# A streamed relu-and-sum: partition pitches of 60 KB and 452 KB in place of 512 KB, and early sums stored by SyncE

## The chip, the cores and the metric

The kernel runs on one core of a Trainium2 chip. The metric is device time in microseconds (us) of one execution. Most executions of one kernel agree within 0.3%.

A ratio below is the mean time of one kernel's fast runs over the mean time of the other's fast runs of the same rounds, so it is not quite the ratio of the medians that stand beside it. An interval is the 95% interval of that ratio.

## The reference

```python
def setup_inputs():
    batch, seq, dim = 32, 512, 1024
    return {"x": np.random.randn(batch, seq, dim).astype(np.float32)}

def reference(x):
    relu_x = np.maximum(x, 0)
    return np.sum(relu_x, axis=-1).astype(np.float32)
```

These are 16,384 rows of 4 KB, 67.11 MB of input, and one float per row of output. Each of the 128 partitions gets 128 rows.

## The kernel before

Each partition owns 128 consecutive rows, so its data in HBM starts 128 x 4 KB = 512 KB after that of the partition before it. That distance is the pitch. SyncE issues all loads: seven chunks of 16 rows a partition in two buffers, then 8, 4, 2 and 1 rows, then the last row in four pieces. ACT and DVE reduce alternate rows.

```python
xv = x_flat.rearrange("(p m) d -> p (m d)", p=P)              # pitch 512 KB
out2d = out.rearrange("b s -> (b s)").rearrange("(p m) -> p m", p=P)
big, tail, pieces = 16, [8, 4, 2, 1], [244, 252, 260, 268]    # (three lines, shortened)
# ... cut: pools, act_op and dve_op (relu with a running sum into one column of res)
for j, cpd in enumerate(chunks):
    # ... cut: xt = a tile of cpd rows; 8 rows and more from the two "io" buffers
    nc.sync.dma_start(out=xt, in_=xv[:, m0 * D : (m0 + cpd) * D].rearrange("p (c d) -> p c d", c=cpd))
    for c in range(cpd):
        m = m0 + c
        if m == NT - 2:
            act_op(xt[:, c, :], xt[:, c, :], m)
            nc.scalar.dma_start(out=out2d[:, 0 : NT - 2], in_=res[:, 0 : NT - 2])
        elif (c % 2) == 0:
            act_op(xt[:, c, :], xt[:, c, :], m)
        else:
            dve_op(xt[:, c, :], xt[:, c, :], res[:, m : m + 1])
    m0 += cpd
# ... cut: four pieces of the last row, loaded by SyncE and summed by DVE
nc.sync.dma_start(out=out2d[:, NT - 2 : NT], in_=res[:, NT - 2 : NT])
```

The scheduler puts ACT's store ahead of its last row, since the store needs only the first 126 columns.

## Time and profile before

| | before |
|---|---|
| median of the first 3 runs | 163.6 us (163.25 to 163.61) |
| span in the profile | 161.5 us |
| input at 433.7 GB/s (pace of the median 64 KB packet) | 154.7 us |
| first load packet starts, last one ends | 1.02 us, 158.12 us |
| DVE's last operations | 157.58 to 159.18 us |

The first view is the profile's page of the kernel before: the busy time of the two computing engines, the DMA rows in 40 equal slices (tenths of busy time, then GB/s), the DMA queues (packets, MB, share of the 16 engines' time), and the chain of waits that ended last.

```profile
span 161.5 us, 347 instructions
DVE 74.3 (46%) x134; ACT 69.0 (43%) x129; POOL 0.2 (0%) x4
...
DMA  8997997996997997997996997997997997999990
GB/s 308 471 503 308 487 487 308 503 503 292 503 503 308 487 503 325 471 519 308 471 519 296 487 503 325 471 503 341 454 503 341 454 503 308 430 438 406 406 359 22
...
q1 hardware_dynamic: 2304, 67.11, 96.9%
q10 hardware_dynamic: 144, 0.06, 0.1%
q14 instruction: 2, 0.02, 0.0%
...
DMA 79%; DVE 18%; SPq 1%; issue 0%; DVEq 0%
DMA xt<-in_x_dram 62%; DVE xt L79 17%; DMA p<-in_x_dram 17%; SPq L95 1%; DVE p L79 1%; DVEq L79 0%; DVEq L16 0%
```

The DMA engines are busy 96.9% of the span with the loads, and neither computing engine reaches half. The swing between 300 and 500 in the GB/s row is no real swing: a 64 KB packet lasts 2.4 us and a slice 4.0 us, so a packet counts wholly in one slice. The rate has to be read from packets: the trace's record of each packet gives 896 packets of 64 KB with a median of 2.418 us, and 16 x 65,536 bytes / 2.418 us is 433.7 GB/s. The 17% of "DVE xt" in the chain are releases of a buffer; they do not delay the stream, because the other buffer's load is still running.

The second view is the timeline at the end of the kernel before (start in us, duration in us, engine and operation; in brackets the idle time before it and what ended it).

```profile
157.27 0.37 ACTq L103 DMA_DIRECT2D out_dram<-res  x1
157.58 0.41 DVE L79 TENSOR_SCALAR_CACHE_REDUCE p<-p 128x244 f32<-128x244 f32 x1 [0.40 <-DMA p<-in_x_dram]
...
158.64 0.19 ACT L71 ACTIVATION_READ_ACCUMULATOR xt<-xt 128x1 f32 x1
158.74 0.43 DVE L79 TENSOR_SCALAR_CACHE_REDUCE p<-p 128x271 f32<-128x271 f32 x1
...
159.25 0.35 SPq L128 DMA_DIRECT2D out_dram<-res  x1
```

DVE starts the first piece when it lands, works without a break to 159.18 us, and the last store follows. ACT ends at 158.83 us, 0.35 us ahead of DVE, although it spends 0.37 us on issuing its store.

### The profile page before, as it was taken

What the parts mean: (1) busy time and instruction counts of PE and PEld (TensorE: products, weight loads), DVE (VectorE), ACT (ScalarE), POOL (GpSimd) and SP (SyncE); (2) the same over time, 40 slices, a digit from 0 to 9 for tenths busy, and PEclk for the clock granted to TensorE, in tenths of its full rate; (3) what the DMA queues carried; (4) which work ended last, traced back from release to release, by engine and by line L of the source; (5) the groups of instructions that cost most, each with busy time, mean ns of one, the idle gap of its engine ahead of it and who ended that gap; (6) DMA issues with size and microseconds to landing.
All of it is one profiled execution on the core that took longest, in us unless ns stands there. A gap on an engine that the chain in (4) does not pass through costs nothing.

```text
span 161.5 us, 347 instructions
## 1 busy us (share of the span) xinstructions
DVE 74.3 (46%) x134; ACT 69.0 (43%) x129; POOL 0.2 (0%) x4
## 2 busy tenths in 40 slices
DVE  0000049700695008940099101991039900598983
ACT  3000049500693008920099001990039700596882
POOL 0000000000000000000000000000000000000000
DMA  8997997996997997997996997997997997999990
GB/s 308 471 503 308 487 487 308 503 503 292 503 503 308 487 503 325 471 519 308 471 519 296 487 503 325 471 503 341 454 503 341 454 503 308 430 438 406 406 359 22
DMA packets 2450, 67.19 MB, mean 416 GB/s; under 512 B 528, under 2 KB 1040, under 8 KB 1168
## 3 DMA queue, kind: packets, MB, share of 16 engines
q1 hardware_dynamic: 2304, 67.11, 96.9%
q10 hardware_dynamic: 144, 0.06, 0.1%
q14 instruction: 2, 0.02, 0.0%
HBM read 67.11 MB, written 0.07 MB: 416 GB/s over the span
## 4 chain that ended last, share of the span: by engine, by line
DMA 79%; DVE 18%; SPq 1%; issue 0%; DVEq 0%
DMA xt<-in_x_dram 62%; DVE xt L79 17%; DMA p<-in_x_dram 17%; SPq L95 1%; DVE p L79 1%; DVEq L79 0%; DVEq L16 0%
## 5 line engine op out<-in xcount | busy, mean ns | idle before, releaser
L79 DVE TENSOR_SCALAR_CACHE_REDUCE xt<-xt 128x1024 f32<-128x1024 f32 x63 | 72.6, 1216 | 84.5 <-DMA xt<-in_x_dram 84.2
L71 ACT ACTIVATE xt<-xt 128x1024 f32<-128x1024 f32 x64 | 66.7, 1043 | 89.0 <-DMA xt<-in_x_dram 89.0
L71 ACT ACTIVATION_READ_ACCUMULATOR xt<-xt 128x1 f32 x64 | 11.9, 187 | 0.0
L79 DVE DVE_READ_ACCUMULATOR xt<-xt 128x1 f32 x63 | 5.2, 83 | 0.0
L79 DVE TENSOR_SCALAR_CACHE_REDUCE p<-p 128x244 f32<-128x244 f32 (+3 forms) x4 | 1.6, 420 | 0.4 <-DMA p<-in_x_dram 0.4
L71 ACT ACT_TABLE_LOAD x1 | 1.3, 1283 | 0.8 <-PEq L143 0.8
L79 DVE DVE_READ_ACCUMULATOR p<-p 128x1 f32 x4 | 0.3, 82 | 0.0
L143 POOL MEMSET const-bfloat16-1.0<- 128x1 bf16 x1 | 0.1, 101 | 0.0
L143 POOL MEMSET const-uint8-127<- 128x1 uint8 x1 | 0.1, 101 | 0.0
L143 POOL MEMSET const-float32-0.0<- 128x1 f32 x1 | 0.1, 98 | 0.2 <-issue 0.2
L143 POOL MEMSET const-float32-1.0<- 128x1 f32 x1 | 0.1, 98 | 0.0
## 6 DMA issues: line engine op xcount, KB each, us to landing
xt<-in_x_dram SPq DMA_DIRECT2D x1, 4096.0 KB, 19.6
xt<-in_x_dram SPq DMA_DIRECT2D x1, 2048.0 KB, 24.2
xt<-in_x_dram SPq DMA_DIRECT2D x1, 1024.0 KB, 26.2
xt<-in_x_dram SPq DMA_DIRECT2D x1, 512.0 KB, 27.0
p<-in_x_dram SPq DMA_DIRECT2D x1, 134.0 KB, 10.0
p<-in_x_dram SPq DMA_DIRECT2D x1, 130.0 KB, 26.5
p<-in_x_dram SPq DMA_DIRECT2D x1, 126.0 KB, 26.7
p<-in_x_dram SPq DMA_DIRECT2D x1, 122.0 KB, 26.8
```

Of the source, the lines that this page charges most:

```text
L71: nc.scalar.activation(out=out_ap, in_=in_ap, func=mybir.ActivationFunctionType.Relu, accum_out=res[:, m : m + 1],)
L79: nc.vector.tensor_scalar(out=out_ap, in0=in_ap, scalar1=0.0, scalar2=None, op0=mybir.AluOpType.max, op1=mybir.AluOpType.add, accum_out=ac ...
L95: nc.sync.dma_start(out=xt, in_=xv[:, m0 * D : (m0 + cpd) * D].rearrange("p (c d) -> p c d", c=cpd),)
L143: nc = _bacc.Bacc("TRN2", target_bir_lowering=False, num_devices=1)
```

## The change

The intent is to take the pitch off a large power of two. The input is cut into a first block, where each partition has 15 rows (pitch 15 x 4 KB = 60 KB), and the rest, where it has 113 (pitch 452 KB). The first load has 15 rows; six of 16 and loads of 9, 4, 2 and 1 rows follow. The sums exist in two tiles, and SyncE stores the early ones in two transfers after the last load. The core of the diff, shortened:

```diff
-    xv = x_flat.rearrange("(p m) d -> p (m d)", p=P)
-    out2d = out.rearrange("b s -> (b s)").rearrange("(p m) -> p m", p=P)
-    tail = [8, 4, 2, 1]
+FIRST = 15
+TAIL = [9, 4, 2, 1]
+    cut = P * FIRST
+    xa = x_flat[:cut].rearrange("(p m) d -> p m d", p=P)
+    xb = x_flat[cut:].rearrange("(p m) d -> p m d", p=P)
+    # outa and outb likewise
@@ loads
+    nc.sync.dma_start(out=xt[:, :FIRST, :], in_=xa)
+    for n in [BIG] * nbig + TAIL:
+        nc.sync.dma_start(out=xt[:, :n, :], in_=xb[:, m0 : m0 + n, :])
@@ stores
-                nc.scalar.dma_start(out=out2d[:, 0 : NT - 2], in_=res[:, 0 : NT - 2])
+    nc.sync.dma_start(out=outa, in_=resa)
+    nc.sync.dma_start(out=outb[:, : M - 2], in_=resb[:, : M - 2])
 # (cut: tiles, the pieces and the last store, which stay as they were)
```

The 9-row load has a tile of its own; the 8-row load took one of the two large buffers.

More of the change, by code (lines that the diff above doesn't have):

```diff
@@ L10 @@
 EARLY = 1
+FIRST = 15
+BIG = 16
+TAIL = [9, 4, 2, 1]
+PIECES = [244, 252, 260, 268]
 def kernel(tc: tile.TileContext, x: bass.AP, out: bass.AP):
@@ L17, with trace_relu_sum, act, dve @@
     issue_ahead_of_the_barrier(tc, EARLY)
+@with_exitstack
+def trace_relu_sum(
+    ctx: ExitStack,
+    tc: tile.TileContext,
+    x: bass.AP,
+    out: bass.AP,
+):
+    nc = tc.nc
+    fp32 = mybir.dt.float32
+    P = nc.NUM_PARTITIONS
+    x_flat = x.flatten_outer_dims()
+    N, D = x_flat.shape
+    NT = N // P
+    assert N == P * NT and sum(PIECES) == D
+    nbig, rem = divmod(NT - FIRST - sum(TAIL) - 1, BIG)
+    assert rem == 0
+    cut = P * FIRST
+    xa = x_flat[:cut].rearrange("(p m) d -> p m d", p=P)
+    xb = x_flat[cut:].rearrange("(p m) d -> p m d", p=P)
+    out1d = out.rearrange("b s -> (b s)")
+    outa = out1d[:cut].rearrange("(p m) -> p m", p=P)
+    outb = out1d[cut:].rearrange("(p m) -> p m", p=P)
+    io = ctx.enter_context(tc.tile_pool(name="io", bufs=2))
+    small = ctx.enter_context(tc.tile_pool(name="small", bufs=1))
+    resa = small.tile([P, FIRST], fp32)
+    resb = small.tile([P, NT - FIRST], fp32)
+    def act(ap, accum_out):
+        nc.scalar.activation(
+            out=ap,
+            in_=ap,
+            func=mybir.ActivationFunctionType.Relu,
+            accum_out=accum_out,
+        )
+    def dve(ap, accum_out):
+        nc.vector.tensor_scalar(
+            out=ap,
+            in0=ap,
+            scalar1=0.0,
+            scalar2=None,
+            op0=mybir.AluOpType.max,
+            op1=mybir.AluOpType.add,
+            accum_out=accum_out,
+        )
+    def rows(xt, n, res, m0):
+        for c in range(n):
+            (act if c % 2 == 0 else dve)(xt[:, c, :], res[:, m0 + c : m0 + c + 1])
+    xt = io.tile([P, BIG, D], fp32, tag="io", name="first")
+    nc.sync.dma_start(out=xt[:, :FIRST, :], in_=xa)
+    rows(xt, FIRST, resa, 0)
+    m0 = 0
+    for n in [BIG] * nbig + TAIL:
+        if n == BIG:
+            xt = io.tile([P, BIG, D], fp32, tag="io", name=f"big{m0}")
+        else:
+            xt = small.tile([P, n, D], fp32, name=f"t{n}")
+        nc.sync.dma_start(out=xt[:, :n, :], in_=xb[:, m0 : m0 + n, :])
+        rows(xt, n, resb, m0)
+        m0 += n
+    M = NT - FIRST
+    assert m0 == M - 1
+    np_ = len(PIECES)
+    parts = []
+    col = 0
+    for i, w in enumerate(PIECES):
+        extra = np_ - 1 if i == np_ - 1 else 0
+        pt = small.tile([P, w + extra], fp32, name=f"p{i}")
+        nc.sync.dma_start(out=pt[:, :w], in_=xb[:, M - 1, col : col + w])
+        parts.append(pt)
+        col += w
+    nc.sync.dma_start(out=outa, in_=resa)
+    nc.sync.dma_start(out=outb[:, : M - 2], in_=resb[:, : M - 2])
+    last, w = parts[-1], PIECES[-1]
+    for i in range(np_ - 1):
+        dve(parts[i], last[:, w + i : w + i + 1])
+    dve(last, resb[:, M - 1 : M])
+    nc.sync.dma_start(out=outb[:, M - 2 :], in_=resb[:, M - 2 :])
@@ L36, in issue_ahead_of_the_barrier @@
     opening[at:at] = loads
-@with_exitstack
-def trace_relu_sum(
-    ctx: ExitStack,
-    tc: tile.TileContext,
-    x: bass.AP,
-    out: bass.AP,
-):
-    nc = tc.nc
-    fp32 = mybir.dt.float32
-    P = nc.NUM_PARTITIONS
-    x_flat = x.flatten_outer_dims()
-    N, D = x_flat.shape
-    assert N % P == 0
-    NT = N // P
-    xv = x_flat.rearrange("(p m) d -> p (m d)", p=P)
-    out2d = out.rearrange("b s -> (b s)").rearrange("(p m) -> p m", p=P)
-    big = 16
-    tail = [8, 4, 2, 1]
-    pieces = [244, 252, 260, 268]
-    assert sum(pieces) == D
-    nbig, rem = divmod(NT - sum(tail) - 1, big)
-    assert rem == 0
-    chunks = [big] * nbig + tail
-    io_pool = ctx.enter_context(tc.tile_pool(name="io", bufs=2))
-    res_pool = ctx.enter_context(tc.tile_pool(name="res", bufs=1))
-    res = res_pool.tile([P, NT], fp32)
-    def act_op(in_ap, out_ap, m):
-        nc.scalar.activation(
-            out=out_ap,
-            in_=in_ap,
-            func=mybir.ActivationFunctionType.Relu,
-            accum_out=res[:, m : m + 1],
-        )
-    def dve_op(in_ap, out_ap, accum_out):
-        nc.vector.tensor_scalar(
-            out=out_ap,
-            in0=in_ap,
-            scalar1=0.0,
-            scalar2=None,
-            op0=mybir.AluOpType.max,
-            op1=mybir.AluOpType.add,
-            accum_out=accum_out,
-        )
-    m0 = 0
-    for j, cpd in enumerate(chunks):
-        if cpd >= 8:
-            xt = io_pool.tile([P, cpd, D], fp32, tag="io", name=f"xt{j}")
-        else:
-            xt = io_pool.tile([P, cpd, D], fp32, tag=f"t{cpd}", bufs=1, name=f"xt{j}")
-        nc.sync.dma_start(
-            out=xt,
-            in_=xv[:, m0 * D : (m0 + cpd) * D].rearrange("p (c d) -> p c d", c=cpd),
-        )
-        for c in range(cpd):
-            m = m0 + c
-            if m == NT - 2:
-                act_op(xt[:, c, :], xt[:, c, :], m)
-                nc.scalar.dma_start(out=out2d[:, 0 : NT - 2], in_=res[:, 0 : NT - 2])
-            elif (c % 2) == 0:
-                act_op(xt[:, c, :], xt[:, c, :], m)
-            else:
-                dve_op(xt[:, c, :], xt[:, c, :], res[:, m : m + 1])
-        m0 += cpd
-    m_last = m0
-    assert m_last == NT - 1
-    base = m_last * D
-    np_ = len(pieces)
-    wlast = pieces[-1] + (np_ - 1)
-    ptiles = []
-    col = 0
-    for i, w in enumerate(pieces):
-        shape_w = w if i < np_ - 1 else wlast
-        pt = io_pool.tile([P, shape_w], fp32, tag=f"p{i}", bufs=1, name=f"p{i}")
-        ptiles.append(pt)
-        nc.sync.dma_start(out=pt[:, 0:w], in_=xv[:, base + col : base + col + w])
-        col += w
-    last = ptiles[-1]
-    for i in range(np_ - 1):
-        dve_op(ptiles[i], ptiles[i], last[:, pieces[-1] + i : pieces[-1] + i + 1])
-    dve_op(last, last, res[:, m_last : m_last + 1])
-    nc.sync.dma_start(out=out2d[:, NT - 2 : NT], in_=res[:, NT - 2 : NT])
```

## The prediction

> **What bounds it now.** The input stream. The profile's DMA row is at 9 tenths or more in nearly all 40 slices; the chain of waits is 79% DMA and 18% DVE; DVE is busy 46%, ACT 43%. In the packet records of the trace 896 packets of 64 KB carry the big loads, median 2.418 us each; 16 engines at that pace are 433.7 GB/s. So 67.11 MB need 154.7 us; the first packet starts at 1.02 us and the last piece's packets end at 158.12 us. Only about 2.4 us of the stream is not at full pace. Then come the DVE's piece sums (chain: 157.58 to 159.18 us), the last store, and the end at 161.5 us.
>
> **The intent, costed.** The pitch between partitions is now 512 KB. The Trainium skill, page "DMA: Bandwidth & Descriptors", section "Latency and other measured facts", lists 207 GB/s per direction at a 512 KiB pitch against 214 with a padded one, about 3%. This trace does not show that loss: the same page ("Where 436 GB/s comes from") gives a ceiling of 435 GB/s, and the median packet runs at 433.7. What could be pitch is the packets over 2.5 us, 26 of 896: the first on each engine takes about 3.0 us (2.55 to 3.24), 0.6 us too long; seven more, near 11.3 to 12.1 us, average 0.2 us too long. I think the first packet pays a start-up latency, not the pitch: the following packets keep the spacing and the offsets between engines, yet take 2.42 us. Were it all pitch, the stream would gain 0.6 to 0.9 us.
>
> **What moves.** The first load has 15 rows (60 KB a partition), then six of 16, then 9, 4, 2, 1 and the pieces; from the 9-row chunk on the landings come where they came before (148.6, 153.5, 155.95 us). A 16-row chunk takes 9.2 us to reduce and 19.4 us to load, so buffers come free in time. The 9-row chunk no longer waits for a buffer; that gains nothing, since the queue is never empty. ACT gets five of its rows instead of four and starts the 4-row chunk 0.5 us late, but no longer issues the 63 KB store (0.37 us at 157.27 us): it ended at 158.8 us, now about 158.4. DVE ended at 159.18 us, so ACT is off the path.
>
> SyncE issues two early stores, near 148.7 us (7.5 KB) and 157.3 us (55.5 KB), 0.35 us each, and is idle again before the DVE's end. Their packets (eight each per engine; one of 504 bytes took 28 ns) queue behind the pieces and should be done before the last store's, at about 160.1 us. Cost on the path: 0 to 0.2 us.
>
> **Sum.** 163.4 minus 0 to 0.6 (start) plus 0 to 0.2 (stores): 163.2 us, range 162.4 to 163.9. Chances: faster by over 2% 0.02, within 2% 0.95, slower 0.03.
>
> **What will show it.** 64 KB packets keep a median of 2.42 us; the first packets, now 60 KB (2.27 us at full pace), still take 2.7 to 3.0 us (if about 2.3, the pitch was the cause); the first piece lands at 157 to 157.6 us; DVE still ends the chain; both early stores end before the last is issued; span 161 to 161.6 us.
>
> **What would make it wrong.** The new pitches hit HBM worse than 512 KB (64 KB packets well over 2.42 us); early stores delay the pieces' landing or the last store; pitch losses in unprofiled runs that this one trace does not show.

## The result

| | before | after |
|---|---|---|
| median | 163.51 us (163.25 to 163.61, 4 runs) | 163.53 us (163.45 to 163.63, 4 runs) |
| ratio | | 1.0004 (0.9986 to 1.0021) |
| span of the profiled run | 161.5 us | 161.8 us |
| last load packet ends | 158.12 us | 158.43 us |

The two kernels take the same time. The page of the kernel after:

```profile
span 161.8 us, 345 instructions
DVE 73.1 (45%) x132; ACT 69.9 (43%) x131; POOL 0.2 (0%) x4
...
DMA  8999989979979979969979979979979989999980
GB/s 289 440 486 471 404 373 518 454 324 518 470 308 518 470 308 518 486 292 518 486 308 490 470 340 486 486 340 486 470 340 486 470 356 420 419 437 404 407 323 19
...
q1 hardware_dynamic: 2592, 67.18, 97.0%
q14 instruction: 2, 0.02, 0.0%
...
DMA 79%; DVE 12%; ACT 5%; SPq 1%; issue 0%; DVEq 0%
```

The DMA's shares are the same; of the chain's computing steps ACT now has 5% and DVE 12% in place of 18%. The queue q10 is gone, since it was ACT's; its bytes now go through SyncE's queue q1. The timeline after:

```profile
148.89 0.35 SPq L102 DMA_DIRECT2D out_dram<-resa  x1
...
157.56 0.34 SPq L103 DMA_DIRECT2D out_dram<-resb  x1
...
157.87 0.41 DVE L64 TENSOR_SCALAR_CACHE_REDUCE p<-p 128x244 f32<-128x244 f32 x1 [0.37 <-DMA p<-in_x_dram]
...
158.53 0.19 ACT L56 ACTIVATION_READ_ACCUMULATOR t<-t 128x1 f32 x1
...
159.03 0.43 DVE L64 TENSOR_SCALAR_CACHE_REDUCE p<-p 128x271 f32<-128x271 f32 x1
...
159.53 0.33 SPq L108 DMA_DIRECT2D out_dram<-resb  x1
```

Everything in this stretch comes 0.3 us later than before (157.87 against 157.58 us, 159.53 against 159.25 us), because the load stream ends 0.3 us later. ACT's slack has grown: it ends at 158.72 us, 0.74 us ahead of DVE, and not 0.35 us.

So the pace of the packets did not change, yet in this profile the end of the stream moved the wrong way. The experiments ask three things: whether the pitch does anything at all, whether the two halves of the change cancel, and what decides when the stream ends.

### The profile page after: what moved, and what is told of

Same layout as the page of the kernel before. It is cut to its first block, busy times and chain, and to the rows that moved or that the text cites. A ratio compares the mean times of both kernels' runs of the same rounds, so it can differ in the third digit from the quotient of the medians.

```text
span 161.8 us, 345 instructions
## 1 busy us (share of the span) xinstructions
DVE 73.1 (45%) x132; ACT 69.9 (43%) x131; POOL 0.2 (0%) x4
## 4 chain that ended last, share of the span: by engine, by line
DMA 79%; DVE 12%; ACT 5%; SPq 1%; issue 0%; DVEq 0%
DMA big<-in_x_dram 37%; DMA p<-in_x_dram 29%; DMA first<-in_x_dram 13%; DVE big L64 11%; ACT first L56 5%; SPq L87 1%; DVE p L64 1%; DVEq L64 0%; DVEq L20 0%
## 5 line engine op out<-in xcount | busy, mean ns | idle before, releaser
L64 DVE TENSOR_SCALAR_CACHE_REDUCE big<-big 128x1024 f32<-128x1024 f32 x48 | 55.2, 1214 | 62.6 <-DMA big<-in_x_dram 62.6
L56 ACT ACTIVATE big<-big 128x1024 f32<-128x1024 f32 x48 | 50.0, 1042 | 66.1 <-DMA big<-in_x_dram 66.1
L64 DVE TENSOR_SCALAR_CACHE_REDUCE first<-first 128x1024 f32<-128x1024 f32 x7 | 8.1, 1217 | 21.4 <-DMA first<-in_x_dram 21.4
L56 ACT ACTIVATE first<-first 128x1024 f32<-128x1024 f32 x8 | 8.3, 1041 | 19.3 <-DMA first<-in_x_dram 19.3
L56 ACT ACTIVATE t<-t 128x1024 f32<-128x1024 f32 x9 | 9.4, 1046 | 2.6 <-DMA t<-in_x_dram 2.4
L64 DVE TENSOR_SCALAR_CACHE_REDUCE t<-t 128x1024 f32<-128x1024 f32 x7 | 8.2, 1217 | 2.0 <-DMA t<-in_x_dram 1.9
L56 ACT ACTIVATION_READ_ACCUMULATOR big<-big 128x1 f32 x48 | 8.9, 186 | 0.0
L64 DVE DVE_READ_ACCUMULATOR big<-big 128x1 f32 x48 | 3.9, 82 | 0.0
L56 ACT ACTIVATION_READ_ACCUMULATOR t<-t 128x1 f32 x9 | 1.7, 187 | 0.0
L56 ACT ACTIVATION_READ_ACCUMULATOR first<-first 128x1 f32 x8 | 1.5, 186 | 0.0
```

Of the source, the lines that this page charges most:

```text
L56: nc.scalar.activation(out=ap, in_=ap, func=mybir.ActivationFunctionType.Relu, accum_out=accum_out,)
L64: nc.vector.tensor_scalar(out=ap, in0=ap, scalar1=0.0, scalar2=None, op0=mybir.AluOpType.max, op1=mybir.AluOpType.add, accum_out=accum_out,)
```

## The experiments

Twelve experiments ran (three of them repeat a kernel). The table holds what the packet records of the traces show for the kernels with large loads. "First packet" is the duration of each engine's first load packet (mean and longest of 16). "Stalls" are later 60 and 64 KB packets that lasted at least 0.08 us over the median of their size, without those that an instruction refill touched (e9_few_ops explains these); their excess is summed and divided by 16.

| kernel | pitch, KB | first packet, us | stalls: number, us an engine | loads end, us | ratio to before |
|---|---|---|---|---|---|
| before | 512 | 3.00, 3.24 | 8, 0.10 | 158.12 | 1 |
| e0_before_again | 512 | 3.06, 3.35 | 7, 0.04 | 158.19 | 1.0004 |
| e2_store_only | 512 | 2.85, 3.30 | 11, 0.13 | 158.20 | 1.0002 |
| e3_chunks_only | 512 | 2.90, 3.07 | 8, 0.07 | 158.14 | 1.0000 |
| e9_few_ops | 512 | 2.97, 3.37 | 7, 0.09 | 157.75 | 0.9991 |
| after | 60, 452 | 3.08, 3.54 | 1, 0.01 | 158.43 | 1.0004 |
| e10_after_again | 60, 452 | 3.07, 3.62 | 2, 0.02 | 158.33 | 1.0015 |
| e1_pitch_only | 60, 452 | 3.06, 3.83 | 1, 0.01 | 158.67 | 1.0024 |
| e11_pitch_again | 60, 452 | 2.96, 3.53 | 0, 0.00 | 158.35 | 1.0011 |
| e4_first16 | 64, 448 | 3.03, 3.29 | 0, 0.00 | 157.90 | 0.9991 |

The median 64 KB packet is 2.418 us in every one of these traces. First packets of 60 KB (after, e1, e3, e10, e11) compare with a later pace of 2.267 us.

### e0_before_again: how far two profiles of one kernel differ

No edit.

> The kernel before, unchanged: it shows how far two profiles of one kernel differ. Both theories: ratio 1.000 within 0.002, about 163.5 us. My theory (the stream runs at the pace of the 16 engines' packets, the pitch costs nothing, the slow first packet is start-up latency): the first packet on each engine again averages 2.8 to 3.2 us, and the mean moves by up to 0.2 us from run to run; the last piece's packets end within 0.3 us of 158.1 us. Rival (the first packet is slowed by the pitch, always alike): its mean comes back within 0.05 us.

Measured: 163.52 us, ratio 1.0004 (0.9991 to 1.0017). The first packets averaged 3.06 us and the loads ended at 158.19 us. All of my theory's figures were met. The rival, an unchanging mean within 0.05 us, came near (3.00 and 3.06 us), so this run only measures the spread. The stalls near 11 us of the first profile did not come back there; here five lay between 35 and 48 us and two near 87 us, and they were smaller.

### e1_pitch_only: the new pitches and ACT's stores

```diff
@@ after
         rows(xt, n, resb, m0)
+        if n == TAIL[0]:
+            nc.scalar.dma_start(out=outa, in_=resa)
+        if n == TAIL[2]:
+            nc.scalar.dma_start(out=outb[:, : NT - FIRST - 2], in_=resb[:, : NT - FIRST - 2])
-    nc.sync.dma_start(out=outa, in_=resa)
-    nc.sync.dma_start(out=outb[:, : M - 2], in_=resb[:, : M - 2])
```

> The new pitches and chunks, but the early sums are stored by ACT as before. Theory 1 (neither part does anything on the critical path): ratio to before 0.998 to 1.002, 163.2 to 163.8 us. Rival (the pitch gains 0.3 to 0.6 us and the stores by SyncE give it back): ratio 0.996 to 0.998, about 163.0 us.

Measured: 163.82 us, ratio 1.0024 (1.0011 to 1.0037). This met neither theory: it is slower, where the rival wanted it faster. In its profile the loads end at 158.67 us and one engine's first packet lasted 3.83 us. The scheduler also moved the store of the first 15 columns forward: its packets ran between 34 and 50 us, amid the loads. A pitch that gains something which SyncE's stores give back is refuted by the sign; that SyncE's stores gain 0.3 us was still possible, and the repeat below decides it.

### e2_store_only: pitch and chunks of before, early sums stored by SyncE

```diff
@@ before
-                nc.scalar.dma_start(out=out2d[:, 0 : NT - 2], in_=res[:, 0 : NT - 2])
@@
+    nc.sync.dma_start(out=out2d[:, 0 : NT - 2], in_=res[:, 0 : NT - 2])
     last = ptiles[-1]
```

> The pitch and the chunks of before, but the early sums are stored by SyncE. Theory 1: ratio 0.998 to 1.002; ACT ends its last row about 0.3 us earlier, DVE still ends the chain. Rival (stores by SyncE cost what the pitch gains): ratio 1.002 to 1.004, with the last store issued later than 159.5 us.

Measured: 163.42 us, ratio 1.0002 (0.9989 to 1.0014). The timeline at its end:

```profile
157.31 0.35 SPq L122 DMA_DIRECT2D out_dram<-res  x1
...
158.29 0.18 ACT L71 ACTIVATION_READ_ACCUMULATOR xt<-xt 128x1 f32 x1
...
159.32 0.34 SPq L128 DMA_DIRECT2D out_dram<-res  x1
```

ACT's last row ends at 158.47 us in place of 158.83 us, as expected, and the last store is issued at 159.32 us, with the same lag behind DVE as before. Who stores the early sums makes no difference to the time: SyncE is free long before DVE ends, and ACT was not the last engine to begin with.

### e3_chunks_only: the new chunks at the old pitch

```diff
@@ before
-    tail = [8, 4, 2, 1]
+    head = 15
+    tail = [9, 4, 2, 1]
-    chunks = [big] * nbig + tail
+    chunks = [head] + [big] * nbig + tail
-        if cpd >= 8:
+        if cpd >= 15:
```

> The chunks of after (15, six of 16, 9, 4, 2, 1) at the pitch of before, 512 KB, with ACT's store: the 15-row load has 60 KB packets 512 KB apart. Theory 1 (start-up latency): its first packet on each engine averages 2.85 to 3.1 us, 0.6 to 0.8 us above the 2.27 us of the later ones, as after at 60 KB pitch; ratio 0.998 to 1.002. Rival (512 KB slows the later first-chunk packets near 11 us, and 60 KB slows the first): first packet about 2.8 us, and again several packets of the first load 0.1 to 0.4 us too long near 11 us.

Measured: 163.47 us, ratio 1.0000 (0.9985 to 1.0015). The first packets averaged 2.90 us, 0.63 us over the later pace of 2.267 us. Theory 1 covers that, and so nearly does the rival (2.8 us); but the rival's stalls near 11 us did not appear. They came at 49 to 54 us instead. The sizes of the chunks do nothing to the time.

### e4_first16: a first block of 16 rows

```diff
@@ after
-FIRST = 15
+FIRST = 16
-TAIL = [9, 4, 2, 1]
+TAIL = [8, 4, 2, 1]
```

> The change with a first block of 16 rows instead of 15: pitches 64 KB and 448 KB, chunks 16, 16, ... 8, 4, 2, 1 as before, early sums stored by SyncE. What the first runs showed: all kernels' engines reach the tail at the same mean time; the end of the loads is set by the slowest engine, which starts up late or slowly and loses 1.1 us near 83 to 87 us while two 8 KB refills of instructions pass it. Theory (the pitch does nothing in steady state): 64 KB packets at a median of 2.418 us again, ratio to before 0.998 to 1.003. If a dense first block slows the first packets unevenly: the longest first packet is again 3.4 us or more, and the loads end at 158.4 us or later. Rival (a 60 KB pitch, not a power of two, is what spares something): first packets slower here than after's mean of 3.08 us, by over 0.3 us.

Measured: 163.30 us, ratio 0.9991 (0.9978 to 1.0005). The longest first packet was 3.29 us, not 3.4 or more, and the loads ended at 157.90 us. So, as far as one profile shows, a dense first block as such does not stretch the first packets, and the rival (over 0.3 us slower first packets at 64 KB) fell too: their mean was 3.03 us. There was no stall. It is the best of the correct kernels, but its interval reaches past 1.

### e5_short_512k and e6_short_452k: loads of four rows, both pitches

```diff
@@ before (e5); e6 has the same chunks on views with 60 and 452 KB pitch, and two early stores by ACT
-    chunks = [big] * nbig + tail
+    chunks = [3] + [4] * 30 + [2, 1, 1]
-            xt = io_pool.tile([P, cpd, D], fp32, tag="io", name=f"xt{j}")
+            xt = io_pool.tile([P, cpd, D], fp32, tag="io", bufs=8, name=f"xt{j}")
```

> The pitch of before, 512 KB, with loads of at most four rows (3, 30 times 4, 2, 1, 1 and the pieces): packets of 16 KB, so that an engine moves to an address 512 KB on four times as often. Theory (bound by the packets' pace, first packet late by latency): 16 KB packets at a median of 611 to 615 us/1000, as in the tail of before; the first packets, 12 KB each (0.46 us at that pace), last 1.0 to 1.4 us, that is a fixed 0.6 to 0.8 us more; the loads end about 0.6 to 1.0 us later than before (31 chunks whose packets carry 7 ns each), 164.0 to 165.0 us. Rival (the 512 KB pitch costs 3% when packets are short): median packet 0.63 us or more, 168 us or more.

> The same short loads with the change's pitches, 60 KB and 452 KB. Theory: within 0.3% of the run with short loads at 512 KB, same median packet. Rival (pitch matters when packets are short): faster than it by 1% to 3%.

Measured: 165.99 us at 512 KB, ratio 1.0169 (1.0139 to 1.0198); 165.38 us at 60 and 452 KB, ratio 1.0123 (1.0104 to 1.0141). The difference is 0.6 us by the medians, between my 0.3% and the rival's 1%. The intervals overlap by a hair (1.0139 to 1.0141), and one of the four runs at 60 and 452 KB (165.90 us) is slower than the fastest at 512 KB (165.86 us), so the times of this pair alone do not settle it. The rival's slower rate is not how it shows: the median 16 KB packet lasted 612 ns in one and 613 ns in the other (the expectations write such times as "us/1000", meaning ns). Reading each trace in stretches of 8 us (stretch, length, busy time of DVE, ACT and POOL, clock, DMA share, GB/s) finds the place. At 512 KB:

```profile
4.00:12.00 8.00, 2.16 (x3) 3.12 (x5) 0.00 (x0) 1.00 1.01 432
12.00:20.00 8.00, 3.80 (x8) 3.44 (x8) 0.00 (x0) 1.00 1.01 410
20.00:28.00 8.00, 3.82 (x7) 3.64 (x7) 0.00 (x0) 1.00 1.01 432
...
36.00:44.00 8.00, 4.41 (x7) 4.24 (x8) 0.00 (x0) 1.00 1.00 410
```

The same stretches at 60 and 452 KB:

```profile
4.00:12.00 8.00, 2.31 (x3) 3.28 (x7) 0.00 (x0) 1.00 1.01 431
12.00:20.00 8.00, 3.65 (x8) 3.29 (x7) 0.00 (x0) 1.00 1.02 436
20.00:28.00 8.00, 4.74 (x8) 4.38 (x8) 0.00 (x0) 1.00 1.02 434
...
36.00:44.00 8.00, 4.13 (x8) 3.78 (x8) 0.00 (x0) 1.00 1.01 430
```

Two stretches are short of bytes at 512 KB although the engines are busy throughout. The packet records show why: at 15.2 to 15.5 us and again at 37.9 to 38.3 us, eight packets in flight together lasted 0.65 to 0.92 us too long. Outside these moments the pace is the same. With the other stalls this is 0.79 us an engine, against none at 60 and 452 KB; the loads end at 160.47 and 159.57 us.

The expectation for the first packets was wrong: 12 KB ones lasted 0.85 and 0.97 us on average and not 1.0 to 1.4 us. The runs were also slower than expected (164 to 165 us), and the loads ended later than expected even without stalls. I had counted the few ns that a 16 KB packet takes over its share of a 64 KB one (612 ns against 2418 / 4 = 604.5 ns) once a load; each engine carries eight packets a load. Over 30 loads that is an estimated 240 x 7.5 ns = 1.8 us in place of 0.2 us.

### e9_few_ops: no instruction refill during the stream

In the kernel before, one DMA engine falls behind all others at 86 us. The profile's queue q14 is labelled "instruction": at 86.35 and 86.65 us two packets of 8 KB ran on it, 0.31 us each. The Trainium skill, page "Runtime: NRT & Kernel Launch", section "Instruction fetch mechanics", says that each sequencer fetches its next instructions through a DMA queue of its own and calls the cost "mostly hidden". Chaining each packet's end to the next one's start separates the 16 engines. My chain put both refills on one engine, which then goes from 0.35 us ahead of the mean to 0.77 us behind it; this is the 1.1 us of the expectations. That chain is doubtful: the first refill ends within 0.01 us of the start of the second, and in the other eight traces with refills during the loads the two ran on two engines, whose place against the mean fell by 0.4 to 0.6 us for the first refill and by 0.7 to 0.9 us for the second. Read so, the two engines here lost 0.5 and 0.8 us. By either reading an engine that carried a refill ended the 64 KB packets, at 138.36 us against a mean of 137.59 us. The edit removes most operations and so the refills. Its result is wrong.

```diff
@@ before
     res = res_pool.tile([P, NT], fp32)
+    nc.gpsimd.memset(res, 0.0)
@@
-        for c in range(cpd):
+        for c in range(4 if cpd == big else cpd):
```

> Wrong result on purpose: the kernel before, which reduces only the first 4 rows of each 16-row chunk, so that ACT and DVE run some 21 operations each instead of 64 and 67. All loads and the whole tail stay. Theory (two refills of instructions near 83 to 87 us stall one DMA engine by 1.1 us, and that engine ends the loads): no 8 KB refill during the stream, no engine more than 0.6 us behind the mean at the end of the 64 KB packets (0.77 before), loads end 0.3 to 0.5 us earlier (157.6 to 157.9 us), ratio 0.9965 to 0.9985. Rival (the refills cost nothing, the end is set by start-up alone): ratio 0.999 to 1.001, loads end at 158.1 to 158.2 us.

Measured: 163.37 us, ratio 0.9991 (0.9979 to 1.0004). The stream behaved as the theory said: no refill while it ran (the next ones came at 162.07 and 163.07 us), the last engine 0.50 us behind the mean and not 0.77, and the loads ended at 157.75 us, 0.4 us earlier than in the four other profiles at 512 KB. But only some 0.1 us of it reached the time, which is within the noise, and the ratio missed the 0.9965 to 0.9985 that I expected. Its timeline and span:

```profile
157.18 0.41 DVE L80 TENSOR_SCALAR_CACHE_REDUCE p<-p 128x244 f32<-128x244 f32 x1 [0.43 <-DMA p<-in_x_dram]
...
158.35 0.44 DVE L80 TENSOR_SCALAR_CACHE_REDUCE p<-p 128x271 f32<-128x271 f32 x1
...
158.94 0.35 SPq L129 DMA_DIRECT2D out_dram<-res  x1
```

```profile
span 161.4 us, 183 instructions
```

DVE ends at 158.79 us, 0.39 us earlier than before, and the span ends 0.1 us earlier. The rest went after the stream: the store is issued 0.15 us after DVE's end in place of 0.06 us, with more waits ahead of it (my cleared tile brought another semaphore), and VectorE passes the closing barrier 0.16 us after the other engines, where in the kernel before they pass it together. The refills that were put off started at 162.07 us, after VectorE had passed at 161.41 us, so they are not shown to be what delayed it; the cause of this delay is open. An early end of the loads is also no proof by itself: e4_first16 ended them at 157.90 us with both refills. What the traces show directly is the set-back of the engine that carries one.

### e7_row_512k and e8_row_452k: loads of one row, both pitches

```diff
@@ e5 (e7) and e6 (e8)
-    chunks = [3] + [4] * 30 + [2, 1, 1]
+    chunks = [1] * 127
-        if cpd >= 3:
+        if m0 < 120:
-            ... tag="io", bufs=8
+            ... tag="io", bufs=24
-            elif (c % 2) == 0:
+            elif (m % 2) == 0:
```

> Loads of one row each (127 and the pieces), pitch 512 KB, packets of 4 KB. The runs with four-row loads showed two moments (15.2 and 37.9 us) in which eight engines' packets lasted 0.7 to 0.8 us too long at 512 KB and none at 60 and 452 KB. Theory (at 512 KB the engines now and then meet on one place of HBM, stall together, and are then out of step for long; the cost is lumps, not a slower rate): the median 4 KB packet is the same as with the new pitches, 159 to 170 ns/1000, and lumps appear again, together 0.5 to 3 us an engine; 0.3% to 2% slower than the run with the new pitches. Rival (the lumps are chance and not the pitch): same time within 0.3%. Rival (a lower rate at 512 KB): median packet over 3% longer.

> Loads of one row each with the new pitches, 60 KB and 452 KB: the control for the run before this one. All theories: 4 KB packets near 0.16 us, as in the tail of before, so some 168 to 175 us if SyncE's issues (0.45 us each, 131 of them) keep up; no moment in which half the engines' packets are several times too long.

Measured: 173.80 us at 512 KB, ratio 1.0633 (1.0610 to 1.0657); 173.11 us at 60 and 452 KB, ratio 1.0598 (1.0581 to 1.0614). The difference is 0.4% by the medians, though the intervals overlap a little (1.0610 to 1.0614). The median 4 KB packet was 161 ns in both, so a lower rate is refuted a second time. The stretches at 512 KB:

```profile
4.00:12.00 8.00, 2.80 (x5) 2.96 (x6) 0.00 (x0) 1.00 0.98 344
12.00:20.00 8.00, 4.01 (x7) 3.45 (x6) 0.00 (x0) 1.00 1.03 414
```

And at 60 and 452 KB:

```profile
4.00:12.00 8.00, 3.68 (x6) 3.58 (x7) 0.00 (x0) 1.00 1.03 417
12.00:20.00 8.00, 3.68 (x6) 3.77 (x7) 0.00 (x0) 1.00 1.03 410
```

At 512 KB the stream loses bytes between 4 and 12 us and then runs level with the other. My expectation that the control would have no moment in which many packets are several times too long was wrong: it has one at the very start, where 19 packets between 1 and 2 us lasted 0.6 us too long on average. Summed over the run the stalls are about 1.4 us an engine at 512 KB and 0.7 us at 60 and 452 KB. That is a second pair with the same sign and nearly the same size (stalls differ by about 0.7 us an engine here and by 0.79 us in the pair with four rows). Neither pair's time is clear of noise alone; that both have the sign and the size of their stalls is the evidence. Each kernel of these pairs has one profile.

### e10_after_again and e11_pitch_again: are 0.3 us real?

No edits: the kernel after and e1_pitch_only, side by side.

> The kernel after, unchanged, beside a repeat of the kernel with the pitches alone: they differ in who stores the early sums and by 0.3 us in their first runs. Theory (the end of the loads hangs on the first packet of the engine that later carries the refills, which differs from compile to compile): ratio to before 0.999 to 1.002; if the longest first packet is 3.4 us or more again, a dense first block of 60 KB pitch does that.

> The new pitches with ACT's stores, unchanged. If the 0.24% of its first run came from the stores by ACT (SyncE's stores gain 0.3 us): again 1.001 to 1.004, and slower than the repeat of after by 0.2 to 0.4 us. If it came from chance at start-up: 0.999 to 1.002, within 0.15 us of the repeat of after.

Measured: after again 163.55 us, ratio 1.0015 (1.0001 to 1.0029); the pitches alone again 163.56 us, ratio 1.0011 (0.9999 to 1.0024). They are 0.01 us apart, so the 0.3 us between their first runs did not come back: it belonged to those runs and not to the stores, and SyncE's stores gain nothing that can be seen. Both have a longest first packet over 3.4 us (3.62 and 3.53 us). All four builds with the 60 KB first block have one of 3.53 us or more and end their loads at 158.33 us or later; all five at 512 KB and the one at 64 KB stay at 3.37 us or less. So this block seems to stretch some first packets and to cost some 0.1% (the four ratios are 1.0004, 1.0015, 1.0024 and 1.0011; two of their intervals include 1). It is not density alone, if the one profile at 64 KB can be trusted, since it shows nothing of it. Why 60 KB does is open.

The theory of e10's expectation, that the end of the loads hangs on the first packet of the engine that later carries a refill, fits all the traces. In all nine that have refills during the loads, the engine that ended the 64 KB packets was one that carried a refill. In the four at 512 KB it came out of its first packet 0.08 to 0.18 us ahead of the mean and ended 0.70 to 0.78 us behind it. In the four with the 60 KB block its first packet lasted 3.47 to 3.83 us, it came out 0.21 to 0.58 us behind the mean, and it ended 1.01 to 1.36 us behind. The mean end of the 16 engines did not move: 136.38 us in e3_chunks_only, 136.32 to 136.35 us in these four. Which engine carries a refill was not varied, so that the pitch makes that engine start badly is not shown. (The traces do not number the engines; the chaining is exact but for engines that end a packet within some 0.01 us of each other.)

## Why the prediction was right

The forecast was 163.2 us, from 162.4 to 163.9; measured were 163.53 us, and "within 2%" held. That class asked little: 2% is 3.3 us, and the largest gain that I gave the pitch was 0.9 us. What counts is the mechanism. Point by point:

- **"This trace does not show that loss."** Right. The median 64 KB packet is 2.418 us at every pitch tried, and short packets too keep their pace (612 and 613 ns, 161 and 161 ns). The 435 GB/s that the Trainium skill gives in "DMA: Bandwidth & Descriptors", section "Where 436 GB/s comes from", as the ceiling of the SBUF ports agrees with 433.7 GB/s in this trace; that the HBM side holds such loads to about 358 GB/s, as the same section says, does not (see the last section). Between stalls, HBM at a 512 KB pitch delivers what the engines can take.
- **"The first packet pays a start-up latency, not the pitch."** The second half is right: the mean was 2.85 to 3.08 us at 512, 64 and 60 KB (for the kernel after 3.08 us, just over the 2.7 to 3.0 us that I named), and the excess over the later pace was 0.43 to 0.64 us at 512 KB, 0.61 us at 64 KB and 0.69 to 0.82 us at 60 KB. The first half is not shown. The excess is not one fixed time: 0.20 and 0.25 us for 4 KB, 0.39 and 0.51 us for 12 KB, up to 0.82 us for 60 and 64 KB. The cause of a slow start is open.
- **The start term, "minus 0 to 0.6".** The term of the sum that was mis-sized. It measured plus 0.13 to 0.55 us: the loads end at 158.33 to 158.67 us in four builds, where they ended at 158.12 to 158.20 us in the four at 512 KB that keep all operations. I had asked only how much the pitch could gain there. It did gain something: the stalls of 0.04 to 0.13 us an engine at 512 KB all but vanish. But the stream ends when its slowest engine ends. That was an engine which carried a refill, and with the 60 KB block it was already 0.21 to 0.58 us behind the mean after its first packet, where at 512 KB it was 0.08 to 0.18 us ahead.
- **"Landings come where they came before."** Late by 0.3 us for the same reason (the first piece's sum starts at 157.87 us, and I had expected its landing at 157 to 157.6 us). The span of 161.8 us lies just outside the 161 to 161.6 us that I named.
- **ACT and SyncE off the path, stores "0 to 0.2".** Right. ACT ended at 158.72 us (I said 158.4), DVE at 159.46 us. The early stores' packets ended at 158.83 us, before the last store was issued at 159.53 us. Stores alone had a ratio of 1.0002.

Where the expected gain went: nearly all of it was never there, as the engines already ran at their pace. What the pitch really costs is stalls in which several engines wait at once; with 64 KB packets they are 0.1 us an engine, and the engine that ends last need not be one that they struck. That the engines fall out of step by a stall, and so do not meet again, would explain why there are so few; it was only argued.

## What to carry to other kernels

Before changing a layout for HBM's sake, read the median duration of one large packet and multiply it out over the 16 engines: if that is already the engines' ceiling, a better layout can win only what isolated stalls cost. A stream ends with its slowest engine, so a slow start and an instruction refill on the same engine add up there, while averages over the engines hide them. How much of that reaches the time has to be measured: in e9_few_ops an end 0.4 us earlier left a gain of some 0.1 us, within the noise. A difference of 0.2% between two builds can be chance although its interval excludes a ratio of 1; repeat the build before explaining it.

## What the Trainium skill lacked or had wrong

- "DMA: Bandwidth & Descriptors", section "Latency and other measured facts", lists 207 GB/s per direction at a 512 KiB pitch against 214 at a 4 MiB pitch padded by 4 KiB, for copies from HBM to HBM. It does not say what loads into SBUF show: here 433.7 GB/s by the median packet at 512, 452 and 448 KB alike. The cost came as isolated stalls of 0.65 to 0.92 us on eight engines at once (16 KB packets), some 0.4% of the time with loads of one or four rows (by medians; neither pair is clear of noise alone), and not as a lower rate. Section "Where 436 GB/s comes from" says that for transfers between HBM and SBUF the HBM side, about 358 GB/s, binds: with one core running it did not (416 GB/s over the whole span, 433.7 GB/s by the median packet).
- "Runtime: NRT & Kernel Launch", section "Instruction fetch mechanics", calls refills mostly hidden and speaks of 16 KiB blocks. Here two packets of 8 KB ran during the stream in every kernel with the large loads and all operations (16 KB together, so this does not refute the size of the block). The section says nothing of the loads beside them: one DMA engine was set back by 0.7 to 0.9 us and another by 0.4 to 0.6 us against the mean. In the time, "mostly hidden" holds as far as was measured: the run without refills had a ratio of 0.9991 (0.9979 to 1.0004).
- No page that I found says how long the first packets of a stream last (the DMA page has a latency to the first byte, not a packet's duration): the first 64 KB packet of each engine lasted 2.85 to 3.06 us on average in the five runs that start with such packets, in place of 2.42 us, at 64 KB pitch as at 512 KB.
